# Attention scores from keys stored once, two heads on the two row halves of TensorE, and softmax weights applied on GpSimd

## The chip, the cores and the metric

The kernel runs on one core of a Trainium2 chip. The metric is the time of the device in microseconds (us), the median of the runs shown. Engines are called as in the profile: PE is TensorE's matmul, PEld its load of weights, DVE VectorE, ACT ScalarE, POOL GpSimd and SP SyncE, which issues the large transfers.

## The reference

A trunk of two layers for one sequence of 256 tokens of width 1024, in float32: native sparse attention (NSA), a feed-forward layer, RWKV-7 time mixing and a second feed-forward layer, each behind an RMS norm and added to the residual. The change touches only the attention. It has 16 heads of 64 in 4 groups of keys and values, and three branches that gates add up. With 256 tokens every block is among the selected ones and the window reaches over all keys, so the selected and the window branch are two plain causal attentions with keys and values of their own:

```python
s_s = jnp.einsum('btghd,bgtnkd->bghtnk', qb, k_sel).astype(jnp.float32) * scale
p_s = jax.nn.softmax(jnp.where(valid_s, s_s, NEG_INF)..., axis=-1)
...
s_w = jnp.einsum('btghd,bkgd->bghtk', qb, kw).astype(jnp.float32) * scale
p_w = jax.nn.softmax(jnp.where(valid_w, s_w, NEG_INF), axis=-1)
o_w = jnp.einsum('bghtk,bkgd->btghd', p_w.astype(vw.dtype), vw)
...
o = gb[..., 0:1] * o_c + gb[..., 1:2] * o_s + gb[..., 2:3] * o_w
```

The third branch, `o_c`, attends to 15 compressed blocks.

## The kernel before

The sequence is two tiles of 128 tokens (t = 0, 1). Large weights come in chunks of 512 KB; ACT and DVE cut each into two parts (`wh`, `wl`), and a product is three matmuls of these parts (`mm3`). Those of the query projection (into `acc`, lines 265 to 267) and of the output projection (into `noa`) have nothing to do with the change, but they are what fills PE between steps of the attention.

The 16 heads go in eight pairs (`pr` = 0 to 7). A pair has two heads s = 0, 1 of two neighbouring groups (`gp` names the pair of groups, `hg` the head in it), so that the queries of head 0 stand transposed on partitions 0 to 63 of `qT` and those of head 1 on 64 to 127. `NSA_ORDER` lists the steps in which the program is traced: K the transposed keys, T the queries, s, w, v the scores, weights and values of a pair, q a part of the query projection, C and P scores and probabilities of the compressed blocks, h and H the compression itself (`hids`, `hrep` and their products `pk`, `pv`), G gates. The engines' final order is made by the scheduler of the framework from that trace; only the order on SP is the written one.

For a pair, **scores** has PE write S0 (first token tile, 128 keys for each of two branches, 256 columns) and S1 (second tile, 512 columns) for each head. Each score runs over all 128 partitions: the keys of each group are stored in a tile of their own whose other half is zero, so the other head's queries add nothing. DVE adds the mask and takes the smallest (L630, with a read of its accumulator), ACT takes the exponential and its sum (L634), DVE makes the weight of a row from the sum and the gate (L637, L639). **weigh** multiplies the exponentials by these weights, on DVE (L649), eight instructions a pair; PE transposes them (L652 to L654, plain 128x128), ACT and DVE copy the transposes out (L656, L659). **values** adds up the compressed branch on 32 rows (L665) and the two others on halves of the columns, one half for each head (L670, L673); ACT and DVE cut the result into `oh` and `ol` (L674, L675).

PSUM has two tags of four banks, "mm" (`pmm`) and "acc" (`pacc`). The scores lie in "mm": in a pair one bank for both S0 and one for each S1. The transposes and the values lie in "acc".

Behind the attention comes the output projection, then its sum is added to `x` (L365), transposed (L299, `m0p`) and cut in two for the feed-forward layer (L302 on ACT, `m0l` at L303 on DVE), whose first products are called `mu`.

Of the kernel before, what the change touches and what calls it, by code (L numbers as in the profile page):

```python
# [33 lines left out]
# per-feature vectors, [128, 8] columns each  # L34
# [5 lines left out]
LAG = 2           # feed-forward tiles between the two products of the MLP  # L40
TAIL = 4          # weight chunks at the end of a product that are used by one token tile after the other
NF = DFF // 128
NPERM, NMID, NSLOT = 12, 18, 29       # 4 KB slots: for all layers, from the first feed-forward layer on, with RWKV's


def _mlp_order():
    """(product, feed-forward tile) in the order of use."""
    o, done = [], 0
    for f in range(NF):
        o.append((0, f))  # L50
        if f >= LAG and done < NF - TAIL:
            o.append((1, done))
            done += 1
    return o + [(1, f) for f in range(done, NF)]


# ---------------------------------------------------------------- host layout
def _consts():
    """Arrays that depend on shapes alone, side by side in one [128, n] block."""
# [20 lines left out]
    # cumulative sums about the middle of a chunk: columns t = -1 .. C-1  # L80
# [91 lines left out]
# ---------------------------------------------------------------- the kernel  # L172
@with_exitstack
def trunk(ctx: ExitStack, tc: tile.TileContext, wb, x_in, wg, cw1k, cw1v, cw2, vecs_in, l1, w2, a2, g2, rows,
# [44 lines left out]
    # ---- weights: streamed in 1 MB chunks, cut into two float32r parts  # L219
# [18 lines left out]
    # 4 KB slots, handed out in program order  # L238
# [24 lines left out]
    def mm3(o, lh, ll, rh, rl, first, last):  # L263
        """o += (lh + ll).T @ (rh + rl), without the product of the two low parts."""
        mm(o, lh, rh, start=first, stop=False)  # L265
        mm(o, lh, rl, start=False, stop=False)  # L266
        return mm(o, ll, rh, start=False, stop=last)  # L267
# [17 lines left out]
    def after_split():  # L285
        """What this block traces on ACT and DVE comes after the last split of a layer's input."""
        es = ExitStack()
        for i_ in last_split:
            es.enter_context(tc.issue_after(i_.ins))
        return es  # L290


    def transposed_split(src, gv, h, l, t, name, cbs=(0, 1)):
        """h + l = (src * g).T, columns of token tile t."""
# [15 lines left out]
    def gemm_parts(hT, lT, evac, ncols, ahead=None):  # L310
        """Token-major product with the next weight chunks, 512 columns at a time."""
# [15 lines left out]
    def out_proj(hT, lT, name, after, tail=TAIL, hold=(), own=2):  # L327
        """x += (hT + lT).T @ the next weight chunks, then after(t): one token tile at a time, from the last chunks on."""
# [29 lines left out]
        for t in range(NT):  # L358
            # the second tile's first half of the columns ends before its second one
# [71 lines left out]
    # ================================================================ NSA  # L431
    def nsa():
        with ExitStack() as es:
            pool = es.enter_context(tc.tile_pool(name="nsa", bufs=1))
            kc = [big([128, 2 * G, 2, DH], f"kc{t}") for t in range(NT)]   # every head twice
# [7 lines left out]
            def rope(a, t, n):  # L443
                """First 16 of every 64 columns of a[:, :n * 64], of token tile t, in place."""
# [58 lines left out]
            # ---- compressed blocks  # L503
# [44 lines left out]
            # gelu, tanh form  # L548
# [38 lines left out]
            # ---- transposed keys and queries  # L587
            att = es.enter_context(tc.tile_pool(name="att", bufs=1))
            qT, kT = [], []          # keys: of a group pair; group (the other one's rows zero), branch, key

            def keys():
                for gp in range(2):
                    kT.append(big([128, 2, 2, S], f"kT{gp}"))
                    for s in range(2):
                        P.memset(kT[gp][(1 - s) * 64:(2 - s) * 64, s], 0.0)
# [4 lines left out]
                    for s in range(2):  # L600
                        V.tensor_copy(kT[gp][s * 64:(s + 1) * 64, s], p[s * 64:(s + 1) * 64])
# [10 lines left out]
            # ---- selected and window branches  # L612
# [3 lines left out]
            def scores(pr):  # L616
                gp, hg = divmod(pr, 4)
                st = att.tile([128, 3, 2, 2, 2], F32, name="st", bufs=3)   # (-max, sum, weight), head, query tile, branch
                es_ = []
                S0s = pmm([128, 2, 2, 128], "S0")  # L620
                for s in range(2):
                    S0 = S0s[:, s]
                    mm(S0, qT[gp][:, hg, 0:128], kT[gp][:, s, :, :128], start=True, stop=True)
                    S1 = pmm([128, 2, S], "S1")
                    mm(S1, qT[gp][:, hg, 128:256], kT[gp][:, s], start=True, stop=True)  # L625
# [16 lines left out]
            def weigh(pr, st, es_):  # L642
                pt0 = []
                p1 = pacc("p1").rearrange("p (s b q) -> p s b q", s=2, b=2)
                for s in range(2):
                    e0, e1 = es_[s]
                    for t, e in ((0, e0), (1, e1)):
                        for b in range(2):
                            V.tensor_scalar(e[:, b], e[:, b], st[:, 2, s, t, b:b + 1], None, op0=ALU.mult)  # L649
# [27 lines left out]
            # ---- compressed branch: probabilities, gated, for all heads  # L677
            pcT = att.tile([128, 2, S], F32, name="pcT")     # (hg, s, n), group pair, query
# [33 lines left out]
            # a, q weights and product, in parts, of a half of the queries; l, h, H first layer's weights, hidden units and blocks  # L712
            # of the compression; G gates; K, T transposed keys and queries; C, P scores and probabilities of the compressed
            # blocks; s, w, v scores, weights and values of a pair of heads
# [44 lines left out]
    # ================================================================ RWKV-7  # L759
    def rwkv_weights():  # L760
        """Low-rank weights, the first ones also times the mix of their input; asked for a layer ahead."""
# [13 lines left out]
    def rwkv_input(wts):  # L775
        """Normalised input, transposed, its shift, the keys' mix and the first low-rank products."""
# [55 lines left out]
    def mixed_split(hd, v, h, l, k, t=None):  # L832
        """h + l = hn + dx * mix for one token tile of four feature tiles, or all tokens of two."""
# [11 lines left out]
    def rwkv(inp):  # L845
        hn, dx, xkh, xkl, w2t, a2t, lo = inp
        with ExitStack() as es:
# [6 lines left out]
            hk = pool.tile([128, 3, KT], F32, name="hk")            # a0 / 2, k_a / 2, 1 - k_a / 2  # L854
# [4 lines left out]
            rki = pool.tile([128, KT, H], F32, name="rki")         # r_k of each head in its column  # L859
# [12 lines left out]
            # ---- low-rank parts of the decay, of a and of the gate  # L872
# [25 lines left out]
            # ---- keys  # L898
# [15 lines left out]
            # Heads of the first four feature tiles have the rows that their solutions take (A, B) on partitions 0..63  # L914
            # and those of the values (K) on 64..127; the other heads the other way round.
            AR = [big([128, 2, NCH, 2, C], f"AR{i}") for i in range(4)]   # feature tile, chunk, (A, R), t
            BK = [big([128, 2, NCH, 2, C], f"BK{i}") for i in range(4)]   # feature tile, chunk, (B, K) or (K, B), s
# [3 lines left out]
            rn = pool.tile([128, 32], F32, name="rn")          # -1 / (2 |k k_k|^2): t; chunk, feature tile, head of the pair  # L921
            rnB = pool.tile([128, 32], F32, name="rnB")        # one 32-block to a partition
# [10 lines left out]
            pn = pacc("pn", [128, NCH, 4, 2])      # |k k_k|^2  # L933

            def key_tile(k):
# [4 lines left out]
                act(th, pa, AF.Tanh, scale=0.5, bias=hk[:, 0, k:k + 1])      # 2 a - 1  # L940
                # decays about the middle of each chunk
# [14 lines left out]
                V.scalar_tensor_tensor(th1, th, 1.0, kk, op0=ALU.add, op1=ALU.mult)      # 2 a k; rn has the other half  # L956
# [376 lines left out]
```

## Time and profile before

| | us |
|---|---|
| median of 3 runs (761.9 to 764.71) | 762.09 |
| span of the profiled execution | 758.7 |
| PE busy | 742.6 (98%) |
| DVE busy | 468.5 (62%) |
| ACT busy | 422.7 (56%) |
| POOL busy | 61.1 (8%) |

The profiled execution leaves its span, from the first to the last instruction; a time of its own outside of the profile is not listed. The median of the runs is 3.4 us above the span, which stands for what lies around it. The shares are averages over the whole program; the attention's stretch from the first score to the last values is 69.8 to 144 us.

### The profile page before, as it was taken

The page shows a single profiled execution, that of the slowest core. Times are in us where ns is not written, and L with a number is a line of the kernel's source. Part 1 is how long each engine was busy: PE and PEld are TensorE (multiplying, and loading weights), DVE is VectorE, ACT ScalarE, POOL GpSimd, SP SyncE. Part 2 cuts the span into 40 slices and gives each one's busy share as a digit, 9 for nine tenths or more (in the row PEclk, how much of TensorE's full clock was granted, in tenths as well). Part 3 has the DMA queues.
Part 4 walks back from the last instruction along what each step waited for, and adds up shares of the span by engine and source line. Part 5 has one row for each costly group of instructions (what it writes and reads, how often), then busy time and mean ns, then how long its engine had stood idle before and what let it go on. Part 6 is the DMA issues. An engine that isn't in the chain of part 4 may idle for free.

```text
span 758.7 us, 13485 instructions
## 1 busy us (share of the span) xinstructions
PE 742.6 (98%) x5286; PEld 634.4 (84%) x5286; DVE 468.5 (62%) x963; ACT 422.7 (56%) x870; POOL 61.1 (8%) x77
## 2 busy tenths in 40 slices
PE   7999999999999999999999999999999999999996
PEld 5876866789989989888898885798989889989995
DVE  5767798358454455567856698546667444544553
ACT  6627587247555555563656642444729465565562
POOL 1000000000000000001012610136110000000000
PEclk9999999999999999999999999699999999999999
DMA  8956200218565555680152261320315655555531
GB/s 285 333 172 223 86 27 11 78 53 320 188 191 192 176 190 194 206 280 16 42 181 68 85 189 34 108 98 17 113 55 176 212 187 182 188 185 181 189 112 55
DMA packets 32013, 111.51 MB, mean 147 GB/s; under 512 B 3629, under 2 KB 4141, under 8 KB 31950
## 3 DMA queue, kind: packets, MB, share of 16 engines
q1 hardware_dynamic: 30590, 107.89, 42.7%
q10 hardware_dynamic: 1216, 2.24, 1.1%
q8 instruction: 41, 0.67, 0.4%
q0 software_dynamic: 144, 0.52, 0.2%
q14 instruction: 22, 0.18, 0.1%
HBM read 108.54 MB, written 1.05 MB: 144 GB/s over the span
## 4 chain that ended last, share of the span: by engine, by line
PE 96%; DVE 1%; issue 1%; DMA 1%; ACT 1%; SPq 0%; POOLq 0%; POOL 0%; ACTq 0%; DVEq 0%
PE mu L266 8%; PE mu L265 8%; PE mu L267 8%; PE mo L267 8%; PE mo L265 8%; PE mo L266 8%; PE acc L266 3%; PE acc L265 3%; PE acc L267 3%; PE pa L266 2%; PE pa L265 2%; PE pa L267 2%; PE S L625 2%; PE pM L1037 2%; PE po L670 1%; PE pL L975 1%
## 5 line engine op out<-in xcount | busy, mean ns | idle before, releaser
L231 DVE TENSOR_TENSOR wl<-wst,wh 128x1024 fp32r<-128x1024 f32 x175 | 214.3, 1229 | 177.2 <-ACT wh L229 176.4
L229 ACT ACTIVATE wh<-wst 128x1024 fp32r<-128x1024 f32 x175 | 184.4, 1058 | 166.7 <-PE mu L266 77.5
L266 PE MATMUL mo<-wl,mqh 128*128 128x512 f32 x224 | 88.4, 395 | 0.0
L265 PE MATMUL mo<-wh,mqh 128*128 128x512 f32 x224 | 88.2, 395 | 0.0
L267 PE MATMUL mo<-wh,mql 128*128 128x512 f32 x224 | 87.5, 397 | 0.0
L266 PE MATMUL mu<-m1l,wh 128*128 128x256 f32 x256 | 72.4, 284 | 0.0
L265 PE MATMUL mu<-m0h,wh 128*128 128x256 f32 x256 | 71.5, 281 | 0.4 <-DVE m0l L303 0.4
L267 PE MATMUL mu<-m1h,wl 128*128 128x256 f32 x256 | 71.8, 281 | 0.0
L265 PE MATMUL mu<-m1h,wh 128*128 128x256 f32 x256 | 71.6, 283 | 0.0
L266 PE MATMUL mu<-m0l,wh 128*128 128x256 f32 x256 | 71.6, 281 | 0.0
L267 PE MATMUL mu<-m0h,wl 128*128 128x256 f32 x256 | 71.5, 280 | 0.0
L267 PEld LDWEIGHTS mo<-wh,mql 128*128 128x128 f32 x224 | 42.1, 188 | 9.9
L266 PEld LDWEIGHTS mu<-m1l,wh 128*128 128x128 f32 x256 | 49.0, 191 | 1.1
L265 PEld LDWEIGHTS mu<-m0h,wh 128*128 128x128 f32 x256 | 48.1, 189 | 1.8 <-DVE m0l L303 0.6
L266 PEld LDWEIGHTS mu<-m0l,wh 128*128 128x128 f32 x256 | 48.3, 189 | 1.3 <-DVE m0l L303 0.2
L265 PEld LDWEIGHTS mu<-m1h,wh 128*128 128x128 f32 x256 | 48.2, 190 | 1.2
L266 PEld LDWEIGHTS mo<-wl,mqh 128*128 128x128 f32 x224 | 42.4, 189 | 8.2
L267 PEld LDWEIGHTS mu<-m1h,wl 128*128 128x128 f32 x256 | 49.1, 192 | 0.0
L265 PEld LDWEIGHTS mo<-wh,mqh 128*128 128x128 f32 x224 | 42.0, 188 | 7.8
L267 PEld LDWEIGHTS mu<-m0h,wl 128*128 128x128 f32 x256 | 48.3, 189 | 0.0
L265 PE MATMUL acc<-wh,n0h 128*128 128x512 f32 x80 | 31.8, 404 | 0.0
L267 PE MATMUL acc<-wh,n0l 128*128 128x512 f32 x80 | 31.4, 395 | 0.0
(365 smaller groups left out, 1577.9 us busy)
## 6 DMA issues: line engine op xcount, KB each, us to landing
wst<-in_wb_dram SPq DMA_DIRECT2D x188, 512.0 KB, 3.9
w1t<-in_cw1k_dram SPq DMA_DIRECT2D x4, 512.0 KB, 6.6
w1t<-in_cw1v_dram SPq DMA_DIRECT2D x4, 512.0 KB, 7.6
x<-in_x_dram SPq DMA_DIRECT2D x4, 256.0 KB, 5.0
rowt<-in_rows_dram ACTq DMA_DIRECT2D x2, 512.0 KB, 4.4
VS<-vt ACTq DMA_DIRECT2D x8, 128.0 KB, 2.4
out_dram<-xg SPq DMA_DIRECT2D x4, 256.0 KB, 2.1
g<-in_l_dram SPq DMA_DIRECT2D x2, 320.0 KB, 5.5
```

Source lines behind the costliest of these rows:

```text
L229: act(wh, st, AF.Copy)
L231: V.tensor_tensor(wl, st, wh.bitcast(F32), op=ALU.subtract)
L265: mm(o, lh, rh, start=first, stop=False)
L266: mm(o, lh, rl, start=False, stop=False)
L267: return mm(o, ll, rh, start=False, stop=last)
L625: mm(S1, qT[gp][:, hg, 128:256], kT[gp][:, s], start=True, stop=True)
L670: mm(po[s * 64:(s + 1) * 64, :S], vv[:, 0, vs], pt0[s][:, b], start=False, stop=False)
L975: mm(p[rows_of(k0), c, j], BK[k0 // 2][rs, j, c, k0 // 4], AR[k0 // 2][rs, j, c, 0], start=True, stop=True)
L1037: mm(p[:, j], BK[k // 2][rs, k % 2, c].rearrange("p a s -> p (a s)"), AR[k // 2][rs, k % 2, c].rearrange("p a s -> p (a s)"), start=True, ...
```

## The change

The keys of a pair of groups are stored once, group 0 on partitions 0 to 63 and group 1 on 64 to 127, without zeros; one copy of the transposes replaces two, and four memsets fall away. A score runs over the 64 partitions of its own head, which puts the matmul on one row half of the array; the four scores of a pair are traced in an order in which the halves alternate. Each of them has a bank of its own, so that a pair takes all four of "mm". The weights are applied on POOL. The diff also strips comments; behind line 594 lines shift: 623 and 625 change places (S1 is L623 and S0 is L625 then), L649 becomes L651, L652 to L654 become L654 to L656, L670 and L673 become L672 and L675.

```diff
@@ keys()
-                    kT.append(big([128, 2, 2, S], f"kT{gp}"))
-                    for s in range(2):
-                        P.memset(kT[gp][(1 - s) * 64:(2 - s) * 64, s], 0.0)
+                    kT.append(big([128, 2, S], f"kT{gp}"))
...
-                    for s in range(2):
-                        V.tensor_copy(kT[gp][s * 64:(s + 1) * 64, s], p[s * 64:(s + 1) * 64])
+                    V.tensor_copy(kT[gp], p)
@@ scores(pr)
-                S0s = pmm([128, 2, 2, 128], "S0")
+                S0s = [pmm([128, 2, 128], "S0") for _ in range(2)]
+                S1s = [pmm([128, 2, S], "S1") for _ in range(2)]
+                for s, t in ((0, 0), (1, 1), (0, 1), (1, 0)):
+                    rs = slice(s * 64, (s + 1) * 64)
+                    if t:
+                        mm(S1s[s], qT[gp][rs, hg, 128:256], kT[gp][rs], start=True, stop=True)
+                    else:
+                        mm(S0s[s], qT[gp][rs, hg, 0:128], kT[gp][rs, :, :128], start=True, stop=True)
                 for s in range(2):
-                    S0 = S0s[:, s]
-                    mm(S0, qT[gp][:, hg, 0:128], kT[gp][:, s, :, :128], start=True, stop=True)
-                    S1 = pmm([128, 2, S], "S1")
-                    mm(S1, qT[gp][:, hg, 128:256], kT[gp][:, s], start=True, stop=True)
+                    S0, S1 = S0s[s], S1s[s]
@@ weigh(pr, st, es_)
-                            V.tensor_scalar(e[:, b], e[:, b], st[:, 2, s, t, b:b + 1], None, op0=ALU.mult)
+                            P.tensor_scalar(e[:, b], e[:, b], st[:, 2, s, t, b:b + 1], None, op0=ALU.mult)
```

The engines' order is made by the scheduler, so it moves. First PE at the first two pairs, before (the names are output and inputs with the tile's number; x4 counts equal instructions, behind the shape, columns last; L609 are the transposed queries, L567 transposes the hidden units of the compression):

```order
L609 MATMUL qTp<-cst,q 128x128 x8
L623 MATMUL S_674<-kT_484,qT_660 128x256
L625 MATMUL S_676<-kT_484,qT_660 128x512
L625 MATMUL S_689<-kT_484,qT_660 128x512
L623 MATMUL S_744<-kT_484,qT_660 128x256
L623 MATMUL S_674<-kT_484,qT_660 128x256
L625 MATMUL S_746<-kT_484,qT_660 128x512
L625 MATMUL S_759<-kT_484,qT_660 128x512
L567 MATMUL pht<-cst,gy 128x128 x2
L623 MATMUL S_744<-kT_484,qT_660 128x256
L573 MATMUL pk<-hids,w2t 64x64 x4
L583 MATMUL pv<-w2t,hrep 128x64 x4
```

and with the change:

```order
L606 MATMUL qTp<-cst,q 128x128 x8
L625 MATMUL S_668<-kT_484,qT_654 128x256
L623 MATMUL S_671<-kT_484,qT_654 128x512
L623 MATMUL S_670<-kT_484,qT_654 128x512
L625 MATMUL S_669<-kT_484,qT_654 128x256
L625 MATMUL S_739<-kT_484,qT_654 128x256
L623 MATMUL S_742<-kT_484,qT_654 128x512
L623 MATMUL S_741<-kT_484,qT_654 128x512
L625 MATMUL S_740<-kT_484,qT_654 128x256
L567 MATMUL pht<-cst,gy 128x128 x2
L573 MATMUL pk<-hids,w2t 64x64 x4
L583 MATMUL pv<-w2t,hrep 128x64 x4
```

The scores of the two pairs now stand in one piece, in the alternating order, and the transposes of `gy` behind all of them. On DVE, the rows in front of `hids` at the same place, before:

```order
L630 ISA e_762,st<-S_759,cst 128x256
L630 ISA st 128x1
L630 ISA e_762,st<-S_759,cst 128x256
L630 ISA st 128x1
L637 RECIPROCAL st<-st 128x8
L568 COPY hids<-pht 128x256
L630 ISA e_761,st<-S_744,cst 128x128
L630 ISA st 128x1
L630 ISA e_761,st<-S_744,cst 128x128
L630 ISA st 128x1
L639 TENSOR_TENSOR st<-st,gate 128x4 x2
L579 COPY hrep<-hids 128x256 x2
```

and with the change:

```order
L632 ISA e_758,st<-S_742,cst 128x256
L632 ISA st 128x1
L632 ISA e_758,st<-S_742,cst 128x256
L632 ISA st 128x1
L632 ISA e_757,st<-S_740,cst 128x128
L632 ISA st 128x1
L639 RECIPROCAL st<-st 128x8
L632 ISA e_757,st<-S_740,cst 128x128
L632 ISA st 128x1
L568 COPY hids<-pht 128x256
L641 TENSOR_TENSOR st<-st,gate 128x4 x2
L579 COPY hrep<-hids 128x256 x2
```

Each ISA row with S is a reduce (L630, L632 now), the row behind it the read of its accumulator. The two last reduces of pair 1, which stood between `hids` and `hrep`, now stand ahead of `hids`. The second place is PE among the scores of pairs 4 to 6 (S_1019 to S_1022, S_1148 to S_1151 are pairs 4 and 5 of the changed kernel; p are transposes, e exponentials), before:

```order
L654 MATMUL p_1093<-cst,e_965 128x128 x2
L623 MATMUL S_1149<-kT_494,qT_933 128x256
L625 MATMUL S_1151<-kT_494,qT_933 128x512
L652 MATMUL p_1111<-cst,e_964 128x128
L653 MATMUL p_1111<-cst,e_965 128x128
L652 MATMUL p_1111<-cst,e_964 128x128
L653 MATMUL p_1111<-cst,e_965 128x128
L708 MATMUL pcp<-cst,ce_986 128x128 x2
L665 MATMUL po<-pcT,vcr 128x256
L670 MATMUL po<-pt_1105,ks 64x256
L625 MATMUL S_1164<-kT_494,qT_933 128x512
L623 MATMUL S_1209<-kT_494,qT_933 128x256
```

and with the change:

```order
L623 MATMUL S_1022<-kT_491,qT_929 128x512
L654 MATMUL p_1110<-cst,e_961 128x128
L623 MATMUL S_1021<-kT_491,qT_929 128x512
L625 MATMUL S_1020<-kT_491,qT_929 128x256
L655 MATMUL p_1110<-cst,e_962 128x128
L656 MATMUL p_1092<-cst,e_962 128x128
L654 MATMUL p_1110<-cst,e_961 128x128
L625 MATMUL S_1148<-kT_491,qT_929 128x256
L655 MATMUL p_1110<-cst,e_962 128x128
L656 MATMUL p_1092<-cst,e_962 128x128
L710 MATMUL pcp<-cst,ce_983 128x128 x2
L623 MATMUL S_1151<-kT_491,qT_929 128x512
```

Where two or three scores stood among transposes of the full array's shape, single scores of a row half stand there now, four pieces in eleven rows. The third place is the end of the output projection on PE, before:

```order
L266 MATMUL noa_1483<-wl_1542,oh_1066 128x512
L299 MATMUL m0p<-cst,x 128x128 x4
L267 MATMUL noa_1483<-wh_1540,ol_1068 128x512
L265 MATMUL noa_1483<-nowh,oh_1066 128x512
L299 MATMUL m0p<-cst,x 128x128 x4
L266 MATMUL noa_1483<-nowl,oh_1066 128x512
L267 MATMUL noa_1483<-nowh,ol_1068 128x512
L265 MATMUL noa_1483<-nowh,oh_1066 128x512
L266 MATMUL noa_1483<-nowl,oh_1066 128x512
L267 MATMUL noa_1483<-nowh,ol_1068 128x512
L299 MATMUL m0p<-cst,x 128x128 x8
L265 MATMUL mu<-m0h_1446,wh_1669 128x256
```

and with the change:

```order
L265 MATMUL noa_1485<-nowh,oh_1065 128x512
L266 MATMUL noa_1485<-nowl,oh_1065 128x512
L267 MATMUL noa_1485<-nowh,ol_1067 128x512
L265 MATMUL noa_1485<-nowh,oh_1065 128x512
L266 MATMUL noa_1485<-nowl,oh_1065 128x512
L267 MATMUL noa_1485<-nowh,ol_1067 128x512
L299 MATMUL m0p<-cst,x 128x128 x16
L265 MATMUL mu<-m0h_1448,wh_1671 128x256
```

All sixteen transposes of `m0p` stand behind the last product of `noa` now; eight of them stood among the products. DVE at the same place, before:

```order
L365 TENSOR_TENSOR x<-x,noa_1456 128x512
L365 TENSOR_TENSOR x<-x,noa_1476 128x512
L365 TENSOR_TENSOR x<-x,noa_1463 128x512
L303 SCALAR_TENSOR_TENSOR m0l_1448<-m0p,vec,m0h_1446 128x128 x2
L303 SCALAR_TENSOR_TENSOR m0l_1449<-m0p,vec,m0h_1447 128x128
L365 TENSOR_TENSOR x<-x,noa_1483 128x512
L303 SCALAR_TENSOR_TENSOR m0l_1448<-m0p,vec,m0h_1446 128x128
```

and with the change:

```order
L365 TENSOR_TENSOR x<-x,noa_1458 128x512
L365 TENSOR_TENSOR x<-x,noa_1478 128x512
L365 TENSOR_TENSOR x<-x,noa_1465 128x512
L365 TENSOR_TENSOR x<-x,noa_1485 128x512
L303 SCALAR_TENSOR_TENSOR m0l_1450<-m0p,vec,m0h_1448 128x128
L303 SCALAR_TENSOR_TENSOR m0l_1451<-m0p,vec,m0h_1449 128x128
L303 SCALAR_TENSOR_TENSOR m0l_1450<-m0p,vec,m0h_1448 128x128 x2
```

The last sum into `x` stood behind three of the `m0l`, and now stands ahead of all of them.

## Rows read from the trace of the kernel before

**Rows 1.** The page: busy us, share, instructions; the chain that ended last.

```profile
PE 742.6 (98%) x5286; PEld 634.4 (84%) x5286; DVE 468.5 (62%) x963; ACT 422.7 (56%) x870; POOL 61.1 (8%) x77
...
PE 96%; DVE 1%; issue 1%; DMA 1%; ACT 1%; SPq 0%; POOLq 0%; POOL 0%; ACTq 0%; DVEq 0%
```

**Rows 2.** Busy us by stretch (instructions); granted clock, DMA share, GB/s at the end.

```profile
69.80:78.50 8.70, 7.64 (x40) 5.04 (x41) 7.95 (x49) 7.90 (x34) 0.00 (x0) 1.00 0.11 43
78.50:98.00 19.50, 19.50 (x113) 16.30 (x112) 15.41 (x56) 11.43 (x24) 0.00 (x0) 1.00 0.33 110
98.00:115.00 17.00, 17.00 (x90) 9.79 (x90) 16.93 (x92) 14.38 (x53) 0.00 (x0) 1.00 0.00 1
115.00:144.00 29.00, 29.00 (x195) 19.75 (x194) 19.69 (x87) 16.48 (x56) 0.00 (x1) 1.00 0.12 38
```

**Rows 3.** Timeline, PE, first scores: start us, us, operation, [idle before <-releaser].

```profile
69.83 0.67 PE L623 MATMUL S<-kT,qT 128*128 128x256 f32 x2 [0.34 <-ACT qT L610]
70.33 1.88 PE L625 MATMUL S<-kT,qT 128*128 128x512 f32 x4
72.05 1.03 PE L623 MATMUL S<-kT,qT 128*128 128x256 f32 x4
72.91 1.88 PE L625 MATMUL S<-kT,qT 128*128 128x512 f32 x4
...
76.07 0.46 PE L573 MATMUL pk<-hids,w2t 128*64 128x64 f32 x8 [0.62 <-DVE hids L568]
76.93 1.07 PE L583 MATMUL pv<-w2t,hrep 128*128 128x64 f32 x8 [0.41 <-DVE hrep L579]
77.85 0.28 PE L652 MATMUL p<-cst,e 128*128 128x128 f32 x1
```

**Rows 4.** Timeline, PE, a pair's values behind scores.

```profile
101.66 1.88 PE L625 MATMUL S<-kT,qT 128*128 128x512 f32 x4
103.47 0.69 PE L665 MATMUL po<-pcT,vcr 32*128 32x256 f32 x2
104.09 0.65 PE L670 MATMUL po<-pt,ks 128*64 128x256 f32 x4
104.58 0.39 PE L673 MATMUL po<-pt,ks 128*64 128x128 f32 x4
```

**Rows 5.** Timeline, PE, RWKV stage, a product on 64 rows.

```profile
399.21 0.70 PE L939 MATMUL pa<-wa,a2t 64*128 64x256 f32 x2
399.84 0.28 PE L952 MATMUL pn<-cst,sq 128*64 128x2 f32 x2
```

**Rows 6.** Windows of line L1037 alone, 64x128 products on both row halves.

```profile
461.60:462.15 0.55, 0.55 (x5) 0.55 (x6) 1.00 0.14 34
462.15:463.14 0.99, 0.99 (x17) 0.99 (x16) 1.00 0.93 205
463.14:464.34 1.20, 1.20 (x17) 1.08 (x13) 1.00 0.54 120
```

**Rows 7.** Groups on DVE, 69 to 145 us: busy us, mean ns of one | idle before.

```profile
L649 DVE TENSOR_SCALAR e<-e,st 128x256 f32<-128x256 f32 x32 | 9.9, 348 | 0.0
L649 DVE TENSOR_SCALAR e<-e,st 128x128 f32<-128x128 f32 x32 | 7.8, 281 | 0.0
L630 DVE CUSTOM_DVE_ANT_0 e<-S,cst 128x128 f32<-128x128 f32 x32 | 7.8, 286 | 0.7 <-PE S L623 0.6
```

**Rows 8.** Groups on POOL, whole span, columns as in the group above.

```profile
L960 POOL TENSOR_TENSOR BK<-kh,Ei 128x256 f32<-128x256 f32 x8 | 7.5, 943 | 3.6 <-ACT Ei L948 3.4
...
L595 POOL MEMSET kT<- 64x512 f32 x4 | 2.1, 518 | 0.2
...
L860 POOL MEMSET rki<- 128x128 f32 x1 | 0.2, 209 | 0.0
```

**Rows 9.** Timeline, PE, end of the output projection.

```profile
163.98 0.66 PE L299 MATMUL m0p<-cst,x 128*128 128x128 f32 x4 [0.34 <-DVE x L365]
165.03 0.39 PE L265 MATMUL mu<-m0h,wh 128*128 128x256 f32 x1 [0.39 <-DVE m0l L303]
```

## The prediction

> **What bounds the kernel now.** I read the page's first and fourth parts first: TensorE (PE) is busy 742.6 of 758.7 us, and the chain that ended last is PE for 96% of the span [rows 1]. So what counts is whether PE gets less to do, or has to wait. Then I cut the stretch that the change touches, from the first score (69.8 us) to the last values (144 us), into windows [rows 2]. Behind 78.5 PE has no idle time at all: 19.50 of 19.50, 17.00 of 17.00, 29.00 of 29.00 us. The reader should see two things there. DVE is as full as PE between 98 and 115 (16.93 of 17.00), which invites one to take work off it; but since PE never waits in that window, a lighter DVE gives nothing by itself. And the only place where PE waits is 69.8 to 78.5 (7.64 of 8.70). The timeline of that piece [rows 3] names the waits: PE stands 0.62 us for DVE's `hids` copy and 0.41 us for `hrep`, and 0.34 us ahead of the first score for ACT's copy of `qT`. The granted clock is 1.00 all through.
>
> **Keys once (edit 1).** Four memsets of 0.518 us leave POOL [rows 8], and four DVE copies of half the partitions become two of all of them. The first score waits for `qT` and not for the keys [rows 3]: I cost this at nothing, and the worst is also nothing as long as ACT's `qT` stays the last to come.
>
> **Weights on POOL (edit 3).** DVE loses 32 x 0.348 + 32 x 0.281 = 20.1 us of durations (9.9 + 7.8 = 17.7 us of busy time, since starts overlap) [rows 7], 2.2 us a pair. No trace row shows this operation on POOL with these shapes. From below: a memset of 128x128 takes 0.209 us and one of 512 columns 0.518 [rows 8], so 0.8 ns a column; a memset only writes, so 128x128 costs at least 0.21 and 128x256 0.31, 2.1 us a pair (four of each). From above: a two-input TENSOR_TENSOR of 128x256 takes 0.943 [rows 8]; at that price for all eight a pair takes 7.5 us. One tensor is read here, not two, so I take a value between, 0.4 and 0.6, 4.0 us a pair. Pairs 2 to 7 go by between 98 and 144 us [rows 2], 7.7 us each with the products of the output projection that stand at the end, some 7 us without: POOL, idle there now, keeps up as long as its mean is under 7 / 8 = 0.88 us. I cost it at nothing for PE; what hides it is PE's other work, and above 0.88 it is a rival.
>
> **Scores on row halves (edit 2).** An fp32 score is two passes; a pass of 256 columns takes (72.91 - 72.05) / 4 = 0.215 us and one of 512 takes (72.05 - 70.33) / 4 = 0.43 [rows 3]. A pair has four of each: 2.57 us, and eight pairs 20.6 us. Do two halves of the array work at once? For column halves yes: four passes of 0.215 take 104.58 - 104.09 = 0.49 us [rows 4]. For row halves the RWKV stage has the only case, 64x128 at L1037 [rows 6]: where one half alone is used, 5 passes take 0.55 us (0.11 each), where both are, 17 take 0.99 (0.058 each) and the last 17 take 1.20. So a score on 64 rows costs what it did on 128, but two of different heads lie beside each other, and a pair whose four scores are issued together would take 1.29 us. In the built order they rarely are. Pairs 0 and 1 stand together (the first place shown of the order). Later ones are cut up by transposes (the second place): counted through the order, there are 15 visits of the row mode, the first with eight scores (2.57 us), and behind it eight visits whose longer half is one 512-column score (0.86), two in which one half has both sizes (1.29) and four with a 256-column score (0.43), 11.2 us together, where six pairs cost 15.4 before. That is 2.57 us less in the first visit and **4.3 us less** behind it.
>
> **Changes of the array's shape.** Before, scores and transposes both used the full array; now each visit leaves it and comes back. What a change costs is shown: four L625 passes are worth 1.72 us, but from their start to that of the 32-row matmul it takes 103.47 - 101.66 = 1.81, so 0.09 to get in; its two passes are worth 0.43 and take 104.09 - 103.47 = 0.62, so 0.19 to get out and into the next shape [rows 4]. L939 on 64 rows reads the same: 399.84 - 399.21 = 0.63 for two passes of 0.215 [rows 5]. A change thus costs between 0.09 and 0.2; summed over the stretch's 34 runs of one shape, work by these prices plus the waits and 0.16 to 0.17 a change gives back the 74 us that it takes, so I take 0.17. In the changed order there are 62 runs of one shape, 28 more, 27 of them behind the first visits: **+4.6 us** (2.4 to 5.4). The Trainium skill (TensorEngine Tiling (Array Packing), Key Properties) says that changing the tiling mode drains the engine while tiles of one mode work independently; the rows agree with both halves of that, and without the drain the sum would be 4.6 us lower.
>
> **Values.** Column halves, too, are now parted more often: 10 lone matmul groups on one half instead of 4, **+1.3 us** (6 x 0.215).
>
> **Where the early gain goes.** The 2.57 us saved in the first visit end in front of `hids`. PE already waits there for DVE, which still makes the same reduces one after the other and then `hids` and `hrep`; on DVE the two small reduces that stood between `hids` and `hrep` now stand ahead of both (0.286 us each [rows 7]). So PE's `pk`, which waits for `hids`, comes up to 0.57 us later, and `pv` and the first transposes behind it later by something between that and nothing, as `hrep` itself isn't later: I take **+0.3**. The 2.57 us turn into waiting.
>
> **The end.** 23 more products of the output projection (40 instead of 17) now stand ahead of the last values, as filler; they are only moved. But the third place of the order has all 16 `m0p` transposes behind the last of them, where eight were between, and on DVE the last residual add ahead of every `m0l`. PE waits there now 0.34 and 0.39 us [rows 9], and from the last four transposes to the first `mu` are 1.05 us; I take **+0.5** (0 to 1.05).
>
> **Sum.** -4.3 + 4.6 + 1.3 + 0.3 + 0.5 = +2.4 us on the span of 758.7, so 761.1. The median of the runs stands 3.4 us above the profiled span: **764.5 us**, +0.3%. With the ends of the change price and of the last term: 761.8 to 765.9. 0.5% (3.8 us) is about what a measurement of this kernel tells from no change: under 758.3 is faster, over 765.9 slower.
>
> **Rivals.**
> *A, the changes cost nothing for row halves* (the load of the next weights lies under the running matmul): for it, the entry price of 0.09; against it, 0.19 and 0.2 on the way out. Without them 764.5 - 4.6 = 759.9, and if the lone halves of the values also find a partner, 758.6; that is just short of faster, and any part of the early gain that is kept brings it there.
> *B, PE waits for DVE or ACT (the slower side).* A pair's scores now take all four banks of the tag "mm", so the first score of a pair stands on PE behind the reduces of the pair before, and the transposes are queued behind it; the exponentials too come later. Place: 98 to 135 us. For it: ACT is busy 14.38 of 17.00 us between 98 and 115 [rows 2], so little slack is left once DVE is lighter. Against: 23 moved products stand ready to cover the end. Two of the smaller reduces, which free one bank, take 0.57 us [rows 7]; waited for once a pair, over six pairs, that is +3.4: 767.9, and twice 771.3. It decides from 0.25 us a pair.
> *C, POOL's price is above 0.88 us.* At 0.94 a pair takes 7.5 us instead of 7, six pairs +3: 767.5; at 1.0, stretched by DVE's work beside it, +6: 770.5. For it: the TENSOR_TENSOR row. Against: one input less. The Trainium skill (GPSIMD Engine Reference, Specifications) says that POOL shares its SBUF interfaces with VectorE and can contend with it; no row of this case shows the two on these instructions together, so the rule stands open here.
> *D, the row halves don't overlap here* (a score is issued in one shape but one after the other): +4.3 behind the first visit and more visits at their sums, about +6.8: 771. Rows 6 speak against it.
>
> **Chances.** Forecast 0.53, A 0.10, B 0.19, C 0.12, D 0.06. The forecast's own range is 761 to 768, about 0.16 of its 0.53 over 765.9 and 0.02 under 758.3. Of B 0.15, of C 0.10 and all of D are slower; of A 0.06 is faster. That makes faster 0.08, same 0.45, slower 0.47. The range reaches from A to the dearer ends of B and C: 759 to 772.
>
> **What would show it.** Right: L649's successor on POOL at 0.4 to 0.6 us; PE without idle time from about 79 us to the last values; score visits of 0.86 us plus about 0.3 around each; PE's waits between 69 and 79 us (0.34, 0.62 and 0.41 now) grown by about 2.5 us; the last values 5 to 8 us later than 144, with 23 more products ahead of them. Wrong: POOL rows near 1 us with PE waiting for it at the transposes (C), PE waiting in front of scores for reduces (B), pair times that don't shrink (D), or the next shape's matmul starting right behind a score (A).

## The result and the profile after

The changed kernel takes 781.87 us (median of 4 runs, 779.43 to 787.3), the kernel before beside it 762.37. The ratio is 1.0268, 95% interval 1.0226 to 1.0309: slower by 20 us, where 764.5 and at most 772 was forecast. The page of the changed kernel, busy times, granted clock in 40 slices, and the chain:

```profile
PE 753.0 (97%) x5286; PEld 637.1 (82%) x5286; DVE 454.0 (58%) x897; ACT 422.7 (54%) x870; POOL 108.5 (14%) x137
...
PEclk9999997999999999999999999789999999999999
...
PE 92%; DVE 3%; ACT 2%; issue 1%; DMA 1%; POOL 0%; SPq 0%; POOLq 0%; ACTq 0%; DVEq 0%
```

PE is 10 us busier than before, and still the chain holds less of it, 92% for 96% [rows 1]. The windows that answer to [rows 2], with the same columns:

```profile
69.80:78.50 8.70, 5.80 (x38) 3.54 (x37) 7.36 (x45) 8.03 (x33) 1.03 (x2) 1.00 0.13 52
78.50:98.00 19.50, 19.50 (x105) 16.09 (x104) 12.72 (x34) 8.83 (x16) 11.19 (x15) 0.91 0.25 81
98.00:115.00 17.00, 16.79 (x97) 9.33 (x96) 12.50 (x72) 13.95 (x51) 6.15 (x8) 1.00 0.10 33
115.00:135.00 20.00, 18.20 (x73) 8.76 (x72) 7.12 (x41) 11.17 (x44) 19.91 (x28) 0.74 0.00 1
135.00:155.00 20.00, 17.04 (x108) 11.05 (x107) 8.21 (x27) 8.11 (x25) 11.25 (x13) 1.00 0.17 54
```

Before, PE had no idle time between 78.5 and 144 and a clock of 1.00 there. Now it is idle for 1.80 us of 115 to 135 and 2.96 of 135 to 155, and the granted clock is 0.91 and 0.74 in two windows: the array falls to the lower of its two levels, 1.2 GHz. At that level PE reads as busy (19.50 of 19.50), so busy time alone hides it. The piece in the middle, cut out:

```profile
124.40:134.60 10.20, 9.82 (x30) 4.27 (x28) 2.07 (x12) 3.10 (x12) 10.20 (x15) 0.50 0.00 0
```

Four fences follow: POOL's groups by shape, POOL's timeline in the attention, and who waited between 110 and 150 us on DVE and then on PE (waiter <- releaser: us, times, longest).

```profile
L651 POOL TENSOR_SCALAR e<-e,st 128x256 f32<-128x256 f32 x32 | 30.2, 955 | 0.0
L651 POOL TENSOR_SCALAR e<-e,st 128x128 f32<-128x128 f32 x32 | 20.0, 634 | 77.3 <-DVE st L641 75.1 <-PE p L655 2.2
```
```profile
77.47 12.22 POOL L651 TENSOR_SCALAR e<-e,st 128x128 f32<-128x128 f32 x16 [55.90 <-DVE st L641]
103.37 6.15 POOL L651 TENSOR_SCALAR e<-e,st 128x128 f32<-128x128 f32 x8 [13.68 <-DVE st L641]
115.09 25.22 POOL L651 TENSOR_SCALAR e<-e,st 128x128 f32<-128x128 f32 x32 [5.57 <-DVE st L641]
142.49 5.93 POOL L651 TENSOR_SCALAR e<-e,st 128x128 f32<-128x128 f32 x8 [2.18 <-PE p L655]
```
```profile
DVE e L632 <- PE p L654: 2.9, 1, 2.9
DVE e L632 <- POOL e L651: 2.2, 1, 2.2
```
```profile
PE po L667 <- DVE pt L661: 2.0, 1, 2.0
PE S L623 <- DVE st L632: 1.2, 3, 0.5
PE S L625 <- DVE st L632: 0.6, 1, 0.6
```

A weight costs 0.955 us (128x256) and 0.634 (128x128) in the mean, 6.36 us a pair: under the upper bound of 7.5, but well above the 4.0 that was chosen (0.6 and 0.4), and the larger one costs as much as the two-input row of [rows 8]. The pairs don't come evenly: POOL stands idle for 13.68 and 5.57 us, because the row weights (`st`) from DVE aren't there yet, and then has four pairs back to back for 25.22 us. The waits in front of scores are one chain: PE stands in front of scores because DVE's reduces haven't read their banks; the reduces write the exponentials' buffers, five of each size, two and a half pairs; and these come free when POOL has weighted and PE transposed them. The longest single wait, 2.0 us, stands in front of a pair's values, for the copy of its transposes.

PE's timeline at the first scores, which answers to [rows 3], and then at a later visit of the row mode:

```profile
73.16 1.29 PE L623 MATMUL S<-kT,qT 64*128 64x512 f32 x3 [0.69 <-DVE st L632]
...
77.27 0.46 PE L573 MATMUL pk<-hids,w2t 128*64 128x64 f32 x8 [1.96 <-DVE hids L568]
77.65 1.10 PE L583 MATMUL pv<-w2t,hrep 128*128 128x64 f32 x8
78.59 0.28 PE L654 MATMUL p<-cst,e 128*128 128x128 f32 x1
```
```profile
95.96 0.48 PE L625 MATMUL S<-kT,qT 64*128 64x256 f32 x1
95.97 0.69 PE L623 MATMUL S<-kT,qT 64*128 64x512 f32 x1
96.28 0.38 PE L625 MATMUL S<-kT,qT 64*128 64x256 f32 x1
96.50 0.59 PE L623 MATMUL S<-kT,qT 64*128 64x512 f32 x1
97.02 0.44 PE L710 MATMUL pcp<-cst,ce 128*128 128x128 f32 x2
```

`pk` now waits 1.96 us instead of 0.62, the scores of pair 1 wait 0.69 for a bank, and the first transposes come 8.17 us behind the first score (8.02 before). In the visit two scores start 0.01 us apart, and both take 97.02 - 95.96 = 1.06 us, one longer half (0.86) and 0.20 around it.

Where the 21.2 us between the spans lie is read from two windows, in the first fence of the kernel before, in the second of the changed one: from the first score to the first `mu`, and the RWKV stage behind the last product of L1037.

```profile
69.83:165.03 95.20, 93.44 (x527) 67.08 (x527) 68.88 (x295) 56.37 (x179) 0.15 (x2) 1.00 0.16 55
518.70:569.87 51.17, 50.49 (x551) 44.30 (x550) 31.35 (x57) 27.97 (x110) 12.14 (x7) 1.00 0.20 63
```
```profile
70.42:181.80 111.38, 100.74 (x527) 67.22 (x527) 57.78 (x235) 57.22 (x183) 49.67 (x66) 0.94 0.14 46
536.62:591.02 54.40, 52.48 (x552) 45.38 (x550) 31.20 (x57) 27.71 (x110) 11.73 (x7) 0.97 0.18 59
```

In the stretch PE's idle time grew from 95.20 - 93.44 = 1.76 to 10.64 us: +8.9. The clock of 0.94 costs 0.06 x 111.38 = 6.7 if everything at the lower level took twice as long; that is an estimate, and may be too high. What is left, 100.74 - 6.7 - 93.44 = +0.6, is by that estimate PE's own work. Together +16.2. The first score is 0.6 later; the RWKV stage, which the change doesn't touch, takes 54.40 for 51.17, with 1.2 us more idle time and a clock of 0.97 (1.6 us); the rest, 1.2, lies behind the wait in front of `mu`, where the clock falls once more.

### The profile page after: what moved, and what is told of

Its sections match the earlier page's. It is cut to its first block, busy times and chain, and to the rows that moved or that the text cites. A ratio compares the mean times of both kernels' runs of the same rounds, so it can differ in the third digit from the quotient of the medians.

```text
span 779.9 us, 13525 instructions
## 1 busy us (share of the span) xinstructions
PE 753.0 (97%) x5286; PEld 637.1 (82%) x5286; DVE 454.0 (58%) x897; ACT 422.7 (54%) x870; POOL 108.5 (14%) x137
## 4 chain that ended last, share of the span: by engine, by line
PE 92%; DVE 3%; ACT 2%; issue 1%; DMA 1%; POOL 0%; SPq 0%; POOLq 0%; ACTq 0%; DVEq 0%
PE mu L265 8%; PE mu L266 8%; PE mu L267 8%; PE mo L267 7%; PE mo L266 7%; PE mo L265 7%; PE acc L266 3%; PE acc L265 3%; PE acc L267 3%; PE pa L266 2%; PE pa L265 2%; PE pa L267 2%; PE pM L1039 2%; PE S L623 1%; PE po L672 1%
## 5 line engine op out<-in xcount | busy, mean ns | idle before, releaser
L231 DVE TENSOR_TENSOR wl<-wst,wh 128x1024 fp32r<-128x1024 f32 x175 | 214.0, 1228 | 179.3 <-ACT wh L229 178.8
L651 POOL TENSOR_SCALAR e<-e,st 128x128 f32<-128x128 f32 (+1 forms) x64 | 49.5, 794 | 77.3 <-DVE st L641 75.1
L636 ACT ACTIVATE e<-e,st 128x128 f32<-128x128 f32 (+1 forms) x64 | 28.2, 444 | 7.8 <-DVE st L632 7.8
```

Of the source, the lines that this page charges most:

```text
L231: V.tensor_tensor(wl, st, wh.bitcast(F32), op=ALU.subtract)
L636: act(e[:, b], e[:, b], AF.Exp, scale=-1.0, bias=st[:, 0, s, t, b:b + 1], accum_out=st[:, 1, s, t, b:b + 1])
L651: P.tensor_scalar(e[:, b], e[:, b], st[:, 2, s, t, b:b + 1], None, op0=ALU.mult)
```

## The experiments

Ratios are to the kernel before, timed beside each on the same chip. "Stretch" goes from the first score to the first `mu`; idle is its length less PE's busy time, and clock the granted mean. "RWKV" is the stage of that name in the last fences, from the last product of L1037 to the next `mu`.

| kernel | median us | ratio (95%) | stretch | idle | clock | RWKV |
|---|---|---|---|---|---|---|
| before | 760.9 to 762.4 | 1 | 95.20 | 1.76 | 1.00 | 51.17 |
| the change | 781.87 | 1.0268 (1.0226, 1.0309) | 111.38 | 10.64 | 0.94 | 54.40 |
| halves_dve | 770.28 | 1.0112 (1.0082, 1.0141) | 101.39 | 5.51 | 0.95 | 52.91 |
| pool_full | 777.39 | 1.0213 (1.0190, 1.0236) | 107.72 | 8.62 | 0.97 | 52.92 |
| after_eslots | 775.83 | 1.0184 (1.0149, 1.0219) | 108.82 | 8.38 | 0.94 | 51.08 |
| pool_t0 | 774.73 | 1.0178 (1.0132, 1.0224) | 109.10 | 6.10 | 0.89 | 52.90 |
| before_fill | 759.97 | 0.9989 (0.9976, 1.0003) | 94.17 | 0.73 | 1.00 | 51.07 |
| halves_fill | 769.52 | 1.0096 (1.0075, 1.0117) | 101.06 | 4.39 | 0.97 | 51.06 |
| after_fill | 766.83 | 1.0066 (1.0043, 1.0089) | 100.33 | 6.47 | 1.00 | 51.08 |
| pool_fill | 773.22 | 1.0153 (1.0129, 1.0178) | 102.02 | 6.00 | 1.00 | 54.69 |
| before_4b | 765.66 | 1.0050 (1.0032, 1.0068) | 96.62 | 2.62 | 1.00 | 52.97 |
| halves_hold | 771.10 | 1.0111 (1.0082, 1.0140) | 103.01 | 6.60 | 0.95 | 51.64 |
| after_hold | 767.89 | 1.0099 (1.0067, 1.0131) | 108.32 | 10.98 | 0.94 | 51.08 |
| after_dummy | 779.72 | 1.0234 (1.0177, 1.0292) | 110.52 | 10.11 | 0.97 | 51.09 |

The last four columns are those of the one profiled execution, which can lie some us from the median (that of after_hold took 775.56 us, that of halves_fill 766.59); the mean granted clock differs between executions of one kernel, too (0.971 to 0.986 in after_dummy).

The last column matters for what follows. No edit touches the RWKV stage, but the order of PE's instructions in it is that of the kernel before wherever it takes 51.1 to 51.7 us, and another one wherever it takes 52.9 or more. Those 1.8 us, and up to 3.5 where the clock falls there as well, come with the scheduler's order; before_4b, which has neither row halves nor weights on POOL, has them too.

**halves_dve**: the change with the weights back on DVE.
```diff
-    P.tensor_scalar(e[:, b], e[:, b], st[:, 2, s, t, b:b + 1], None, op0=ALU.mult)
+    V.tensor_scalar(e[:, b], e[:, b], st[:, 2, s, t, b:b + 1], None, op0=ALU.mult)
```


> Keys once and row halves as in the change, weights back on DVE. Theory P (POOL's price: 6.4 us a pair, which keeps the buffers of the exponentials, so that reduces, scores and at last PE wait and the clock falls): nearly all of the 20 us comes back, 764 us as forecast without POOL, within 761 to 768; PE's waits between 110 and 145 us are gone, the clock is 1.00 there. Theory R (row halves with four banks a pair are what stalls PE): 775 us or more, scores still wait for DVE's reduces.


About 12 of the 20 us come back, and 8.5 stay (the stretch is 6.2 us longer than before): neither theory's range held, and theory P is a little over half of it.

**pool_full**: the same line the other way round, in the kernel before.


> The kernel before with the weights alone moved to POOL; scores on all 128 rows, three banks a pair. Theory P: slower by 10 to 20 us, 772 to 782, with POOL busy without a break for several pairs, DVE's reduces waiting for POOL and a stretch at the lower clock. Theory R: within 3 us of before, 759 to 765.


In theory P's range, with POOL busy for five pairs without a break (31.60 us) and a lower clock; DVE's reduces waited for the transposes of the weighted exponentials (2.6 us). This one line makes the stretch 12.5 us longer. The parts cost 1.1% and 2.1%, the whole 2.7%: with these intervals it can't be told whether they add up. Its window of the stretch:

```profile
71.20:178.92 107.72, 99.10 (x527) 69.75 (x527) 57.69 (x234) 57.40 (x183) 49.90 (x66) 0.97 0.15 50
```

**after_eslots**: more buffers.
```diff
-    e0 = att.tile([128, 2, 128], F32, name="e0", bufs=5)
-    e1 = att.tile([128, 2, S], F32, name="e1", bufs=5)
+    e0 = att.tile([128, 2, 128], F32, name="e0", bufs=10)
+    e1 = E1[:, s] if pr > 1 else att.tile([128, 2, S], F32, name="e1", bufs=4)
```
`E1` is a 4 KB slot a pair, taken by `big` in scores and given back in weigh.


> The changed kernel with more buffers for the exponentials: ten of the small ones instead of five, and the two large ones of a pair in a slot of their own from the third pair on. Theory P in its form by buffers (DVE's reduces wait for POOL because five buffers hold two and a half pairs): half or more of the loss comes back, 765 to 773, and no reduce waits for POOL. Theory P in its form by pace alone (a pair can't come out faster than POOL's 6.4 us): 776 to 782. Theory R: 780, as the banks are unchanged.


6 us come back, but only 2.6 of them in the stretch (108.82 for 111.38); another 3.3 are in the RWKV stage, whose order is the old one here. Reduces hardly wait for POOL any more (0.2 us for 2.2), as the form by buffers had it, but its time isn't reached: the buffers are a small part at most. PE's loads for the transposes still wait 2.4 us for POOL (5.2 in the change); that POOL's pace is all of the rest isn't shown.

**pool_t0**: 128x256 weights on DVE, 128x128 on POOL.
```diff
-    P.tensor_scalar(e[:, b], ...)
+    (V if t else P).tensor_scalar(e[:, b], ...)
```


> The changed kernel with the weights of the second token tile (128x256) back on DVE, those of the first (128x128) on POOL. Theory P: POOL takes 2.5 us a pair and keeps up easily, 762 to 768. Theory R: 775 or more. If even 2.5 us a pair on POOL stalls the chain by its later answer alone, some 3 to 6 us over the run with all weights on DVE.


Theories P and R both missed: 4 x 0.662 = 2.6 us a pair on POOL, and still 774.7. It is 4.5 us over halves_dve, which the third one had (3 to 6). The idle time fell to 6.10 us, but the clock was 0.89 in the stretch, 0.11 x 109.10 = 12 us: by that estimate the larger loss here.

**before_fill, halves_fill, after_fill, pool_fill**: a part of the query projection fills PE's early waits.
```diff
-    "... s0 a1 h3 s1 w0 H q4 q5 q6 q7 w1 "
+    "... s0 a1 h3 s1 q4 H w0 q5 q6 q7 w1 "
...
-                    next(part)
+                    with tc.issue_after(last_score[0].ins) if last_score else ExitStack():
+                        next(part)
```
`last_score` is the newest 512-column score; pool_fill is before_fill with the weights on POOL.


> The kernel before with one part of the query projection (q4) traced ahead of the compressed blocks and held behind the scores of pair 1, so that PE has products to make where it waits for hids and hrep. Theory W (the waits of 1.03 us between 69.8 and 78.5 are real idle time of the engine that bounds the kernel): 760.5 to 762, about 1 us faster. Theory N (the order of all that follows changes and eats it): 762 or more.

> Row halves and keys once, weights on DVE, with the same filling. Theory C (PE's idle time between 69 and 79 us, 2.65 us, is followed by a stretch at the lower clock, and the saved score time comes to nothing by that): both go, the low stretch near 78 us isn't there, and the time falls from 770 to 763 to 766. Theory N (the later idle time near 100 us and the order count, not this place): 768 or more.

> The whole change with the same filling. Theory P (POOL's pace sets the middle): the low stretch near 80 us goes and with it some 4 us, but PE still waits behind POOL and the lower clock comes there: 774 to 779. Theory C (the early idle time decides all): 765 or less.

> Scores on all rows, weights on POOL, with the filling of the early waits. It completes the four with filling: 760.0 without either, 769.5 with row halves, 766.8 with both. Theory C+P: like the row halves with POOL, 764 to 768, as the early idle time goes and POOL's 6.4 us a pair is nearly covered by 6.5 us of PE's work a pair. If POOL's pace itself stalls PE, 770 to 777.


The kernel before gains nothing that can be told (0.9989, the interval holds 1), though its early waits are gone and the stretch is 1.0 us shorter, as theory W had it. The whole change gains 15 us, near theory C's bound of 765 (its window of the stretch):

```profile
70.08:170.41 100.33, 93.86 (x526) 64.35 (x526) 56.88 (x235) 57.17 (x183) 52.47 (x66) 1.00 0.15 51
```

No lower clock in the stretch, and 4.2 us less idle time: with 6.7 of clock that is the 11 us by which the stretch is shorter. Another 3.3 us are the RWKV stage, in its old order. POOL's price is no lower in it (1.041 and 0.633 us), so 11 of the 16 us that the stretch had lost hang on when PE stands idle and what the clock does, not on POOL's rate alone. The row halves with DVE gained nothing that can be told, against theory C: the early low stretch is gone, but a later one of 6.8 us is there with the filling (from 103.0 us, behind a wait of 1.60 for a bank) and without (from 105.4, behind one of 0.60). pool_fill lies in its second theory's range, but not shown by its cause: its stretch is 6.8 us longer than before, at a clock of 1.00, and 3.5 us of its loss are in the RWKV stage. Over its whole stretch it loses little more than after_fill (102.02 and 100.33 us).

**before_4b**: the kernel before with four banks a pair.
```diff
-                S0s = pmm([128, 2, 2, 128], "S0")
...
-                    S0 = S0s[:, s]
+                    S0 = pmm([128, 2, 128], "S0")
```


> The kernel before with a bank of its own for each of a pair's four scores, nothing else: scores on all 128 rows, weights on DVE. Theory B (the four banks a pair are what makes PE stand in front of scores for DVE's reduces): 764 to 770, with PE waiting for reduces in front of scores between 75 and 125 us. Theory H (it is the row halves' own cost, shape changes and parted values): 759 to 763, no more waits than before.


+0.5%, the lower end of theory B's range, but not its cause: no score waits for a bank, and the stretch is only 1.4 us longer; PE waits 1.1 us for `hids` (0.62 before). Another 1.8 us are in the RWKV stage (52.97 us where before has 51.17), whose order the scheduler also changed. Three banks with row halves weren't tried: the two S0 of a pair would share a bank, and both halves may then write it at the same time. The Trainium skill (TensorEngine Tiling (Array Packing), Restrictions and Gotchas) says that different row tiles can't access one bank simultaneously; no run here shows it.

**halves_hold, after_hold**: a pair's scores are held behind the last transposes traced ahead of them.
```diff
+                with tc.issue_after(last_tr[0].ins) if last_tr else ExitStack():
                     for s, t in ((0, 0), (1, 1), (0, 1), (1, 0)):
```


> Row halves, weights on DVE, with the filling, and each pair's scores held behind the last transposes traced before them, so that fewer of them are cut up. Against the run with the filling alone (769.5 us): if shape changes and parted values (0.2 us each) are what is left, 3 to 5 us less, 764 to 767; if the waits for reduces are, the same or more.

> The whole change with the filling and the same hold. Against the filling alone (766.8 us): 763 to 766 if shape changes are what is left; 768 or more if holding the scores back lets POOL and the exponentials run dry.


No gain that can be told in either. The hold took away few changes of the array's shape (57 became 52 in the one stretch, 60 became 52 in the other), and it brought waits of its own in front of transposes, 2.7 us for DVE's weights in the one and 4.2 for POOL's in the other, so they don't tell what the shape changes cost.

**after_dummy**: 16 transposes of the unit matrix on PE behind the first two pairs' scores, whose result nobody reads.
```diff
+                elif o[0] == "D":
+                    dm = pacc("dm")
+                    with tc.issue_after(last_score[0].ins):
+                        for j in range(16):
+                            nc.tensor.transpose(dm[:, j % 4 * 128:j % 4 * 128 + 128], ident, ident)
```


> The changed kernel with 16 transposes of the unit matrix (1.75 us, their result unused) on PE behind the scores of the first two pairs, where it stands idle for 2.65 us before the first transposes. Theory C (the lower clock follows from PE's idle time there): the low stretch of 3.4 us at 80 us goes although PE gets more to do, and the time falls by 1 to 3 us, 778 to 781, with the low stretches behind POOL at 124 us as they were. If the clock doesn't hang on that idle time, the low stretch stays and the time is 782 or more.


The time, 779.72, is in theory C's range, but it can't be told from the change's either, and theory C's sign failed: the low stretch is still there, 2 us later. The windows show why it is worth having: PE was busy 6.50 of 7.19 us in front of the first transposes, and 3.42 of 3.87 behind, and the clock fell all the same. Below them is the timeline of what PE did there.

```profile
71.04:78.23 7.19, 6.50 (x35) 4.01 (x35) 5.54 (x35) 6.52 (x27) 0.72 (x2) 1.00 0.05 17
78.23:82.10 3.87, 3.42 (x35) 3.13 (x34) 3.04 (x16) 1.45 (x8) 3.87 (x6) 1.00 0.00 0
82.10:85.50 3.40, 3.40 (x13) 3.01 (x13) 2.43 (x8) 0.95 (x2) 3.40 (x5) 0.50 0.00 0
```
```profile
79.38 1.17 PE L583 MATMUL pv<-w2t,hrep 128*128 128x64 f32 x8
80.39 1.99 PE L691 MATMUL sc<-kcb,qT 128*128 128x32 f32 x16
```

What PE did there were narrow products, 64 and 32 columns. So idle time alone isn't what brings the lower clock. The kernel before shows it more plainly, in its RWKV stage, outside of the windows that the prediction read. The clock fell while PE made 125 products of 32 columns in a row, and by the profile PE wasn't idle at all, neither in front of the fall nor behind it:

```profile
475.50 4.24 PE L1108 MATMUL pU<-T,LO 32*32 32x32 f32 x125
```
```profile
462.00:478.80 16.80, 16.80 (x182) 10.45 (x182) 15.80 (x55) 7.54 (x14) 2.38 (x3) 1.00 0.33 95
478.80:495.80 17.00, 17.00 (x185) 11.18 (x184) 5.50 (x7) 6.64 (x9) 2.38 (x3) 0.50 0.20 63
```

## Why the prediction was wrong

- **PE's own work**: right in the sum, its terms not shown one by one. The prediction sums -4.3 - 2.57 + 4.6 + 0.17 + 1.3 = -0.8 us; in after_fill, at a clock of 1.00, PE is busy 93.86 us where before has 93.44, +0.4. The halves overlap (two scores 0.01 us apart, so rival D falls), and a visit costs 0.20 around it. In the stretch the scores by themselves keep PE busy 23.58 us before and 19.60 in after_fill, the transposes and values together 32.44 and 35.01. That the shape changes eat the saved time is thus not shown: in pool_fill, whose scores use the whole array, transposes and values take 36.02.
- **"Where the early gain goes"**: right: 8.17 us to the first transposes for 8.02.
- **Weights on POOL, "keeps up as long as its mean is under 0.88 us"**: this step failed. Its mean was (0.955 + 0.634) / 2 = 0.79, under the line, but costing it at nothing took a rate for an answer, and took the pairs as evenly spaced: POOL was idle for 13.68 and 5.57 us and then had four pairs in a row for 25.22. A pair is held for POOL's whole 6.36 us, where DVE gave it back in 2.5 (four of each in [rows 7]), and PE gets its input later: its loads for the transposes wait 5.2 us for POOL, in part while other work runs, its scores 2.7 us for reduces, and a pair's values 2.0 us. Alone it costs 2.1% (pool_full). How that splits between the later answer, the buffers and the clock stays open; twice the buffers gave back 2.6 us of the stretch. The value chosen for the price was wrong too, and the upper bound for a pair held. The Trainium skill (GPSIMD Engine Reference, Performance versus the Vector engine) puts POOL at 1.96 times the Vector engine's time for a two-input add of 2048 columns; here, with one tensor read, it is 0.955 / 0.348 = 2.7 and 0.634 / 0.281 = 2.3.
- **Rival B**: the place was right, 1.8 us of waits for banks between 110 and 150 us, and the start. It is part of what row halves cost without POOL, 1.1% (halves_dve), where scores wait 1.3 us for reduces. Four banks alone don't bring that wait: before_4b has none in front of its scores, and half of its 0.5% lies elsewhere.
- **What the sum had no term for**: the granted clock. Rows 2 read 1.00 everywhere and the prediction took that for given. By the estimate above it cost 6.7 us in the stretch and 1.6 in the RWKV stage, and the time behind `mu` grew by 1.2. A wait of PE can thus be dearer than its length; in after_fill, with 6.47 us of them and a clock of 1.00, it wasn't.
- **The end**: +0.5 was forecast. PE waits 2.39 us in front of `mu` now, where 0.34 and 0.39 stood [rows 9], +1.7; the order was read rightly and priced too low.
- **The rest of the program**: taken as unchanged; the RWKV stage's +3.2 came with the scheduler's new order there and a clock of 0.97. In halves_fill and after_fill, with the old order, it takes 51.06 and 51.08 us.

Open: what exactly makes the clock fall (the last section), and why after_fill loses no more in the stretch (100.33 us) than halves_fill (101.06) and pool_fill (102.02), which have each only one of its parts; the orders differ in too many places. Of the 6.4 us between pool_fill and after_fill, 3.6 are the RWKV stage. No version beat the kernel before by what a measurement tells.

## What to carry to other kernels

Where one engine is full, count what a change does to that engine's waits before what it frees elsewhere: DVE was as full as PE, and taking work off it to a slower engine lengthened the time until PE had its input. Ask of a moved step not only whether the new engine keeps up in the mean, but how long one answer takes, whether the pieces come evenly, and how many buffers and banks lie between it and the engine that bounds. When PE's clock reads 1.00, allow for a new wait or a run of narrow products to cost more than its length. And before giving a difference to a change, look at the stages that it doesn't touch: here their order moved too.

## What the runs showed of the hardware

POOL's TENSOR_SCALAR on fp32 with a scalar per partition takes 0.92 us for 256 columns and 0.60 for 128, thus (922 - 602) / 128 = 2.5 ns a column and 0.28 us besides. Most of DVE's work beside it hardly matters: the first two rows below are from 115 to 124.4 us, where DVE is busy for 4.87 of 9.40 us, the third from 124.4 to 134.6, where it is for 2.07 of 10.20. One kind does. The next two rows are from 134.9 to 137.9, beside DVE's subtraction L231, which reads two tensors from SBUF; its row stands below them, and the longest single weight in it took 1.97 us. In after_fill the five longest weights (1.12 to 2.81 us) all overlap an L231.

```profile
L651 POOL TENSOR_SCALAR e<-e,st 128x256 f32<-128x256 f32 x6 | 5.5, 922 | 0.0
L651 POOL TENSOR_SCALAR e<-e,st 128x128 f32<-128x128 f32 x7 | 4.1, 602 | 5.6 <-DVE st L641 5.6
L651 POOL TENSOR_SCALAR e<-e,st 128x256 f32<-128x256 f32 x7 | 6.4, 923 | 0.0
L651 POOL TENSOR_SCALAR e<-e,st 128x256 f32<-128x256 f32 x2 | 2.9, 1444 | 0.0
L651 POOL TENSOR_SCALAR e<-e,st 128x128 f32<-128x128 f32 x1 | 1.1, 1114 | 0.0
134.90 2.56 DVE L231 TENSOR_TENSOR nowl<-wst,nowh 128x1024 fp32r<-128x1024 f32 x2 [0.21 <-PE S L625]
```

So rival C's stretching by DVE's work is there, but rare in this kernel. The two row halves of the array start two fp32 scores 0.01 us apart. The lower clock came behind idle time (1.96 us at `hids`, with the narrow products of `pk` and `pv` behind it) and behind narrow products with PE nearly always or always busy (after_dummy, the kernel before), but the same wait of 2.4 us in front of `mu` was followed by it in the change and not in after_fill. The fences show that wait in the change's timeline, the window behind it, and the window behind the first `mu` of after_fill, whose wait is 2.4 us too:

```profile
181.80 0.39 PE L265 MATMUL mu<-m0h,wh 128*128 128x256 f32 x1 [2.39 <-DVE m0l L303]
```
```profile
182.40:185.80 3.40, 3.40 (x19) 3.40 (x18) 1.96 (x4) 3.25 (x7) 0.00 (x0) 0.51 0.00 0
```
```profile
170.41:180.00 9.59, 9.59 (x80) 9.59 (x81) 7.65 (x14) 9.44 (x19) 0.00 (x0) 1.00 0.52 189
```

The Trainium skill (TensorE: Matmul & The Clock Gate, What's actually happening) describes a gate that sets the clock by how busy the engine has been of late. The falls behind idle time agree with it; the fall in the kernel before, with PE busy in 16.80 of 16.80 us by the profile, shows that the profile's busy time doesn't tell it, and no run here settles what does.
